# Two more places for the b gate's raw weights, and one cast tied behind another

## The chip, the cores and the metric

The kernel runs on one core of one Trainium2 chip. The metric is the device time of one execution in microseconds (us), input and output in the chip's memory; lower is better. The engines are named as in the profile: PE is TensorE (matrix products; PEld its weight loads), ACT is ScalarE, DVE is VectorE, POOL is GpSimd and SP is SyncE, whose queue issues most of the loads.

## The reference

Two layers work on 256 tokens of width 1024 in float32. In each, one normalised input h goes through a combined projection, whose parts feed two branches: a gated DeltaNet (branch a) and a differential softmax attention with eight heads (branch b). Each branch has a SiLU gate z, and a sigmoid gate of its own merges it. Cut to what matters here:

```
h = rmsnorm(x, norm_w[l]); proj = h @ w_in[l]
(q_a, k_a, v_a, ab_a, z_a, q_b, k_b, v_b, z_b, gate_a, gate_b) = split(proj)
y_a = gated_delta_branch(q_a, k_a, v_a, ab_a, z_a, ...)
y_b = diff_attention_branch(q_b, k_b, v_b, z_b, ...)   # softmax scores of heads 0 to 7
merged = sigmoid(gate_a) * (y_a @ w_pa[l]) + sigmoid(gate_b) * (y_b @ w_pb[l])
x = x + merged @ w_out[l]
```

## The kernel before

A projection is computed in pieces of 512 output columns. Its 1024 weight rows come in four pairs of 128 rows (`kp` = 0 to 3; the matmul steps are `kt` = 0 to 7, two for each pair). For one pair `weights` (L227) loads a raw tile of 128x1024 float32 (L247, on SP's queue), casts it on ACT to a rounded high part `hi` (L251), and subtracts that on DVE to get the low part `lo` (L253). `proj_tm` (L258) then makes, for each of two token tiles and two steps, three products: high activations by high weights (L267), by low weights (L268), and low activations by high weights (L269). That is twelve matmuls of 128x512 for a pair and 48 for a projection.

The raw tiles rotate through three places (`tag="raw", bufs=3`); a load can go when the subtraction of an earlier pair has read its place. High and low parts rotate through two buffers each ("the ring"): a cast can go when PE has finished the pair that lies there. A pair may be given a home of its own (`homes` in `weights`, `places` in `proj_tm`); its cast then waits only for its load and for that home. `first` names pairs with a home that are queued with high priority all the same. `later` ties the cast or the subtraction of a pair behind another instruction of the same engine. Nobody writes the order on an engine out in full: a scheduler simulates the instructions' times and puts each on its engine's queue when it is ready there, by priority. On the chip every queue then runs in that order, and an instruction that waits holds up those behind it.

The order of the work around the change is: zb, za, gb, ga (z gates and merging gates of the branches), each as two projections, so zb0, zb1, za0, za1, gb0, gb1, ga0, ga1. The attention of branch b is spread among them: for each head `scores` (L914 on PE; maxima on DVE, L922; exponentials on ACT, L924; combination on DVE, L930), `turn` (transposes, L941) and `attend` (weighted sum, L952, and its copy and squares on ACT, L956 and L958). Scores of heads 4 to 7 fall in za0, za1 and gb0. The rotated q and k lie in `qkT` (L463), one tile for heads 0 to 3 and one for heads 4 to 7, in two of the four places of the tag `p8`; the other two hold the activations `hT`. Each is 8 KB a partition. Once their scores are done, the two places of `qkT` come free. In gb1 and ga the kernel also weighs the DeltaNet's q-k products (L654, L686) and merges triangular blocks (`merges`: L776 needs the tile `T`, loaded on SP and POOL at L758, L790 the tile `U`), and the turned output of branch b then takes two places of `p8`.

Before the change the b gate has two homes in the room of `qkT`, `wgb[0]` for the high and low part of gb0's pair 2, and `wgb[1]` for those of gb1's pair 1 (L1062 to L1067). All its raw tiles go through the three ordinary places.

Of the kernel before, what the change touches and what calls it, by code (L numbers as in the profile page):

```python
# [8 lines left out]
F32 = mybir.dt.float32  # L9
F32R = mybir.dt.float32r  # L10
# [7 lines left out]
P = 128  # L18
# [31 lines left out]
def hybrid_encoder(  # L50
# [21 lines left out]
    def pool(name, bufs=1, space=None):  # L72
        kw = {} if space is None else {"space": space}
        return ctx.enter_context(tc.tile_pool(name=name, bufs=bufs, **kw))
# [3 lines left out]
    big = pool("big")  # L78
# [67 lines left out]
    def e4(name, tag):  # L146

        return [big.tile([P, NM, 512], F32, tag=tag, name=f"{name}_{i}", bufs=2) for i in range(2)]
# [72 lines left out]
    def pair(nm):  # L221
        return [big.tile([P, 2, 4, SEQ], F32R, tag="p8", name=f"{nm}_{i}", bufs=4) for i in range(2)]

    def behind(ins):
        return nullcontext() if ins is None else tc.issue_after(ins)

    def weights(w, c0, n, nm, homes=(None,) * 4, ahead=True, later=None, spare=(), held=None, turned=(), first=()):  # L227

        for kp in range(4):
            act, dve = (later or {}).get(kp, (None, None))
            act = mark[nm, act][0] if isinstance(act, int) else act
            with tc.high_priority(offset=HP) if ahead and (homes[kp] is None or kp in first) else nullcontext():
                if homes[kp] is not None:
                    hi, lo = homes[kp] if isinstance(homes[kp], list) else (homes[kp][:, 0], homes[kp][:, 1])
                else:
                    hi = wpool.tile([P, 2, 512], F32R, tag="hi", name=f"hi_{nm}{kp}", bufs=2)
                    lo = wpool.tile([P, 2, 512], F32R, tag="lo", name=f"lo_{nm}{kp}", bufs=2)  # L240
                if kp in spare:
                    raw = work.tile([P, 2, 512], F32, tag="w4a", name=f"raw_{nm}{kp}", bufs=2)
                else:
                    raw = wpool.tile([P, 2, 512], F32, tag="raw", name=f"raw_{nm}{kp}", bufs=3)
                load = (held or {}).get(kp)
                with behind(load):
                    mark["load", nm, kp] = (nc.scalar if load and load.engine != nc.sync.engine else nc.sync).dma_start(  # L247
                        out=raw[:, :, :n],
                        in_=w[kp * 256 : (kp + 1) * 256, c0 : c0 + n].rearrange("(k p) c -> p k c", p=P)).ins
                with behind(act):  # L250
                    high = (V.tensor_copy if kp in turned else S.copy)(hi[:, :, :n], raw[:, :, :n]).ins  # L251
                with behind(dve):
                    mark[nm, kp] = high, V.tensor_tensor(lo[:, :, :n], raw[:, :, :n],  # L253
                                                         hi[:, :, :n].bitcast(F32), ALU.subtract).ins
            for k in range(2):
                yield 2 * kp + k, hi[:, k, :n], lo[:, k, :n]

    def proj_tm(act, w, c0, n, evac, nm, places=(None,) * 4, spare=(), later=None, turned=(), between=None,  # L258
                banks=None, held=None, first=()):

        accs = (banks or banks2)(f"pp_{nm}")
        for kt, hi, lo in weights(w, c0, n, nm, places, later=later, spare=spare, turned=turned, held=held,
                                  first=first):
            for m in range(NM):
                ts_ = slice(m * P, (m + 1) * P)
                o = accs[m][:, :n]
                T.matmul(o, act[kt // 4][:, 0, kt % 4, ts_], hi, start=kt == 0, stop=False)  # L267
                T.matmul(o, act[kt // 4][:, 0, kt % 4, ts_], lo, start=False, stop=False)  # L268
                mark["proj"] = T.matmul(o, act[kt // 4][:, 1, kt % 4, ts_], hi, start=False,  # L269
                                        stop=kt == KT - 1).ins  # L270
                mark["done", nm, kt] = mark["proj"]
        if between:
            between()
        for m in range(NM):
            evac(m, accs[m][:, :n])

    def homes(tags, nm):

        for tag, n in tags:
            t_ = big.tile([P, n, 2, 2, 512], F32R, tag=tag, name=f"w{tag}_{nm}")  # L280
            for k in range(n):
                yield t_[:, k]
# [82 lines left out]
    for l in range(DEPTH):  # L365
# [12 lines left out]
        places = list(homes((("A", 1), ("ktm", 1), ("vtm", 1), ("B", 2)), f"vb{l}"))  # L378
# [4 lines left out]
        later, between, held = {}, None, {}  # L383
        if l == 0:
            later[0] = None, mark["norm", 0][1]

            def between(kt):
                if kt == 2:
                    held[1] = mark["square", 0, 0]
                    later[1] = mark["split", 0, 0]  # L390
                elif kt == 4:
                    tokens(1, mark["square", 0, 1])
                    held[2] = mark["vb00", 0][0]
                elif kt == 6:
                    prenorm(1, xt, wb, 0, (mark["split", 0, 1][0], mark["vb00", 2][1]))
                    later[3] = None, mark["norm", 1][1]
        else:
            later = {1: mark["norm", 0], 2: (mark["norm", 0][0], mark["split", 0, 0][1]), 3: mark["split", 0, 0]}
            mark["later"] = {0: mark["norm", 1], 1: mark["norm", 1]}
        for _ in proj_by_tile(hT, wl, C_VB, evac_v(0), f"vb{l}0", places, later=later,  # L400
                              spare=(1, 3) if l else (), held=held, between=between,
# [280 lines left out]
        def weigh_q(g, c, after):  # L682
            bv = B[:, c, 4 * g : 4 * g + 4]
            with tc.high_priority(offset=HP):
                gp = gram("kq", g, c, 1, after)
                mark["weighed"] = V.tensor_tensor(bv, gp.unsqueeze(2).to_broadcast([P, 4, 2, P]), bv, ALU.mult).ins  # L686
# [276 lines left out]
        def z_part(z, c_base, nm, i):  # L963
            def evac_z(m, ps):
                silu2(z[i][:, m, :], ps)
            proj_tm(hT, wl, c_base + 512 * i, 512, evac_z, f"{nm}{l}{i}",
                    banks=None if i or nm == "za" else banks2_c)
# [6 lines left out]
        for _ in proj_by_tile(hT, wl, C_VB + 512, evac_v(1), f"vb{l}1", places2, spare=range(4),  # L974
                              later={0: mark["split", 1, 1], 1: mark["split", 1, 1], 2: mark[f"k{l}0", 1],
                                     3: mark[f"k{l}0", 2]} if l else
                              {0: (mark["ab"], mark[f"k{l}0", 1][1]), 1: mark[f"k{l}0", 2],
                               2: mark[f"k{l}0", 3], 3: mark[f"k{l}1", 1]},
                              held={} if l else dict.fromkeys(range(2), mark[f"k{l}0", 1][0])):
# [61 lines left out]
                                                   zv[:, j, :], ALU.mult, ALU.mult)  # L1041
                    split_T(yT[i], ov, m, f"{nm}{i}", w=nw_)

        def gate(c_base, nm, tag, between=(None, None), places=((None,) * 4,) * 2, first=()):
            gt = []
            for i in range(2):
                def evac_g(m, ps, i=i):
                    if not gt:
                        gt.extend(e4(nm, tag))
                    S.activation(gt[i][:, m, :], ps, AF.Tanh, scale=0.5)  # L1050
                proj_tm(hT, wl, c_base + 512 * i, 512, evac_g, f"{nm}{i}", places[i], between=between[i],
                        first=first)
            return gt

        def branch(yT, w_, gt, nm, places=(None,) * 4):
            for i in range(2):
# [2 lines left out]
                    V.scalar_tensor_tensor(gs, gs, 1.0, ps, ALU.add, ALU.mult)  # L1059
                proj_tm(yT, w_, 512 * i, 512, evac_p, f"{nm}{i}", (None,) * 4 if i else places)  # L1060

        wgb = [t_.rearrange("p x b t -> p x (b t)").rearrange("p x (k c) -> p x k c", k=2)  # L1062
               for t_ in pair(f"wgb{l}")]
        gtb = gate(C_GB, f"gb{l}", "ev",
                   (lambda: attend(7, turn(7, es[7], place(34)), place(39)),
                    lambda: [weigh_q(n // 2, n % 2, place((39, 42, 44, 47)[n])) for n in range(4)]),
                   ((None, None, wgb[0], None), (None, wgb[1], None, None)), (1, 2))  # L1067
        r0 = small.tile([P, NM, NH], F32, tag="r0", name=f"r0{l}")
        V.reciprocal(r0, s_all[:, :, 0, :].rearrange("p h q -> p q h"))
        rb = small.tile([P, NM, NH], F32, tag="rb", name=f"rb{l}")  # L1070
# [10 lines left out]

        gate_yb(0)
        gta = gate(C_GA, f"ga{l}", "eo", (lambda: gate_yb(1), None))
        branch(ybT, w_pb[l], gtb, f"pb{l}")
        ch = [chunks(0), chunks(1)]
# [44 lines left out]
        def evac_o(i):  # L1130
            def evac(m, ps):
# [6 lines left out]
                later={2: mark[f"pa{l}0", 3], 3: mark[f"pa{l}1", 1]},  # L1138
                held={2: mark["load", f"pb{l}1", 1], 3: mark["load", f"pb{l}1", 3]})
# [4 lines left out]
                              later={0: mark[f"o{l}0", 1], 1: (mark[f"o{l}0", 1][0], mT_split[1]),  # L1144
                                     2: mT_split, 3: mT_split}, spare=(1, 3),
# [51 lines left out]
```

## Time and profile before

| | us |
|---|---|
| median of 3 runs | 769.4 |
| lowest, highest | 768.44, 772.19 |
| the profiled execution, its own time | 770.43 |
| its span in the profile | 768.7 |

| engine | busy us | share of the span |
|---|---|---|
| PE | 749.1 | 97% |
| DVE | 577.7 | 75% |
| ACT | 470.8 | 61% |
| POOL | 126.1 | 16% |

The profile records each instruction with its start and length, in us from the start of the span. A row of the timeline ends in brackets with how long the engine sat idle before it, and what ended that. Matmuls are pipelined: one of 128x512 is recorded as 0.39 us long, though they start 0.23 us apart. The mean clock granted to PE was 0.996 of full speed.

### The profile page before, as it was taken

How to read it: one execution, taken by the hardware profiler on the slowest of the kernel's cores; microseconds unless marked ns; L12 is line 12 of the kernel's file. 1: busy time of each engine (PE TensorE's matmuls, PEld its weight loads, DVE VectorE, ACT ScalarE, POOL GpSimd, SP SyncE). 2: the span in 40 equal slices, each digit the busy share in tenths (PEclk: the TensorE clock that was granted, in tenths of full speed). 3: DMA queues.
4: the chain of work that ended last, by engine and by line, in shares of the span. 5: the costliest groups of instructions: out<-in, count | busy, mean ns of one | idle time of the engine just before them, and what ended most of it. 6: DMA issues, size and time to landing. Idle time of an engine off the chain costs nothing.

```text
span 768.7 us, 13763 instructions
## 1 busy us (share of the span) xinstructions
PE 749.1 (97%) x5158; PEld 641.8 (83%) x5158; DVE 577.7 (75%) x1083; ACT 470.8 (61%) x1012; POOL 126.1 (16%) x187
## 2 busy tenths in 40 slices
PE   7999999999999999999999999999999889999996
PEld 4899889977877889988889889888787678998884
DVE  5696899999876763478577779999998458437782
ACT  5657675668766574645455668556776557565551
POOL 5100451112031111000010025202111310301000
PEclk9999999999999999999999999999999999999999
DMA  7762767775578242557674257768655934335641
GB/s 230 222 197 60 211 210 210 213 219 171 148 191 202 84 139 86 165 192 239 199 226 140 80 167 245 210 186 232 180 167 160 196 111 133 93 110 192 212 144 55
DMA packets 71795, 131.24 MB, mean 171 GB/s; under 512 B 12288, under 2 KB 12752, under 8 KB 71729
## 3 DMA queue, kind: packets, MB, share of 16 engines
q1 hardware_dynamic: 62718, 111.94, 48.7%
q0 software_dynamic: 6304, 15.15, 7.3%
q10 hardware_dynamic: 2706, 3.28, 1.3%
q8 instruction: 40, 0.66, 0.4%
q14 instruction: 27, 0.21, 0.1%
HBM read 123.44 MB, written 6.91 MB: 170 GB/s over the span
## 4 chain that ended last, share of the span: by engine, by line
PE 72%; DVE 13%; DMA 7%; ACT 4%; issue 3%; POOL 0%; SPq 0%; POOLq 0%; DVEq 0%
PE pp_vb L307 4%; DMA raw_gb<-in_w_in_dram 4%; PE pp_o L307 3%; PE pp_qk L268 2%; PE pp_qk L269 2%; PE pp_qk L267 2%; PE pf_v L323 2%; PE pf_k L327 2%; PE pf_v L327 2%; PE pf_k L325 2%; PE pf_v L325 2%; PE pf_k L323 2%; PE pp_ga L267 2%; PE pp_pb L269 2%; PE pp_ga L269 2%
## 5 line engine op out<-in xcount | busy, mean ns | idle before, releaser
L268 PE MATMUL pp_qk<-lo_qk,hT 128*128 128x512 f32 x128 | 50.9, 398 | 0.2
L269 PE MATMUL pp_qk<-hi_qk,hT 128*128 128x512 f32 x128 | 50.1, 391 | 0.0
L253 DVE TENSOR_TENSOR lo_qk<-raw_qk,hi_qk 128x1024 fp32r<-128x1024 f32 x32 | 40.2, 1257 | 9.7 <-ACT hi_qk L251 9.3
L267 PE MATMUL pp_qk<-hi_qk,hT 128*128 128x512 f32 x128 | 45.2, 393 | 0.0
L251 ACT CAST hi_qk<-raw_qk 128x1024 fp32r<-128x1024 f32 x28 | 29.4, 1050 | 23.5 <-PE pp_qk L269 11.1
L924 ACT ACTIVATE es<-sc,mx 128x256 f32<-128x256 f32 x64 | 29.6, 473 | 17.5 <-DVE mx L922 17.5
L253 DVE TENSOR_TENSOR lo_pb<-raw_pb,hi_pb 128x1024 fp32r<-128x1024 f32 x16 | 19.6, 1225 | 26.8 <-ACT hi_pb L251 26.8
L325 PE MATMUL pf_q<-hT,hi_q 128*128 128x256 f32 x128 | 36.2, 286 | 0.0
L323 PE MATMUL pf_q<-hT,hi_q 128*128 128x256 f32 x128 | 36.1, 287 | 0.0
L323 PE MATMUL pf_v<-hT,hi_v 128*128 128x256 f32 x128 | 35.9, 285 | 0.0
L325 PE MATMUL pf_v<-hT,hi_v 128*128 128x256 f32 x128 | 35.8, 284 | 0.0
L323 PE MATMUL pf_k<-hT,hi_k 128*128 128x256 f32 x128 | 35.7, 284 | 0.0
L325 PE MATMUL pf_k<-hT,hi_k 128*128 128x256 f32 x128 | 35.6, 283 | 0.0
L327 PE MATMUL pf_q<-hT,lo_q 128*128 128x256 f32 x128 | 34.9, 285 | 0.0
L327 PE MATMUL pf_v<-hT,lo_v 128*128 128x256 f32 x128 | 34.5, 288 | 0.0
L327 PE MATMUL pf_k<-hT,lo_k 128*128 128x256 f32 x128 | 34.4, 284 | 0.0
L552 DVE SCALAR_TENSOR_TENSOR cvq<-pf_q,cw,cvq 128x254 f32<-128x254 f32 (+1 forms) x64 | 29.9, 476 | 1.9 <-ACT cvq L548 1.4
L251 ACT CAST hi_pa<-raw_pa 128x1024 fp32r<-128x1024 f32 x16 | 16.9, 1055 | 22.2 <-PE pp_pa L269 16.0
L552 DVE SCALAR_TENSOR_TENSOR cvv<-pf_v,cw,cvv 128x254 f32<-128x254 f32 (+1 forms) x64 | 30.0, 477 | 0.1
L268 PEld LDWEIGHTS pp_qk<-lo_qk,hT 128*128 128x128 f32 x128 | 24.0, 188 | 7.2 <-DVE lo_qk L253 2.3
L552 DVE SCALAR_TENSOR_TENSOR cvk<-pf_k,cw,cvk 128x254 f32<-128x254 f32 (+1 forms) x64 | 28.5, 478 | 2.0 <-ACT cvk L548 1.3
L269 PEld LDWEIGHTS pp_qk<-hi_qk,hT 128*128 128x128 f32 x128 | 24.0, 188 | 4.9
(370 smaller groups left out, 2522.4 us busy)
## 6 DMA issues: line engine op xcount, KB each, us to landing
raw_qk<-in_w_in_dram SPq DMA_DIRECT2D x32, 512.0 KB, 3.8
raw_k<-in_w_in_dram SPq DMA_DIRECT2D x16, 512.0 KB, 4.9
raw_q<-in_w_in_dram SPq DMA_DIRECT2D x16, 512.0 KB, 3.7
raw_v<-in_w_in_dram SPq DMA_DIRECT2D x16, 512.0 KB, 3.8
raw_zb<-in_w_in_dram SPq DMA_DIRECT2D x16, 512.0 KB, 3.7
raw_za<-in_w_in_dram SPq DMA_DIRECT2D x16, 512.0 KB, 3.8
raw_gb<-in_w_in_dram SPq DMA_DIRECT2D x16, 512.0 KB, 5.6
raw_ga<-in_w_in_dram SPq DMA_DIRECT2D x16, 512.0 KB, 4.0
```

The lines of the kernel that those rows point to most:

```text
L251: high = (V.tensor_copy if kp in turned else S.copy)(hi[:, :, :n], raw[:, :, :n]).ins
L253: mark[nm, kp] = high, V.tensor_tensor(lo[:, :, :n], raw[:, :, :n], hi[:, :, :n].bitcast(F32), ALU.subtract).ins
L267: T.matmul(o, act[kt // 4][:, 0, kt % 4, ts_], hi, start=kt == 0, stop=False)
L268: T.matmul(o, act[kt // 4][:, 0, kt % 4, ts_], lo, start=False, stop=False)
L269: mark["proj"] = T.matmul(o, act[kt // 4][:, 1, kt % 4, ts_], hi, start=False, stop=kt == KT - 1).ins
L307: mark["proj"] = T.matmul(o, a_, w_, start=kt == 0 and a_ is ah and w_ is hi, stop=kt == KT - 1 and a_ is al).ins
L323: T.matmul(o, hi[:, cs], act[kt // 4][:, 0, kt % 4, :], start=first, stop=False, skip_group_check=True)
L325: T.matmul(o, hi[:, cs], act[kt // 4][:, 1, kt % 4, :], start=False, stop=False, skip_group_check=True)
L327: T.matmul(o, lo[:, cs], act[kt // 4][:, 0, kt % 4, :], start=False, stop=done, skip_group_check=True)
L552: V.scalar_tensor_tensor(ca[:, o0:o1], acc[:, b, o0 + sft : o1 + sft], cw[:, j, cb : cb + 1], ca[:, o0:o1], ALU.mult, ALU.add)
L924: S.activation(es[:, n, qt, :], spv[:, qt, :], AF.Exp, bias=mx[:, n, qt : qt + 1], accum_out=s_all[:, h, n, qt : qt + 1])
```

## The change

Of the two places of `qkT`, the first now takes `rgb`, the raw tiles of gb0's pairs 2 and 3 (through a new argument `raws`); they are no longer loaded into the three ordinary raw places. The high and low part of gb0's pair 2 go through the ring like those of the other pairs. The second place takes `wgb`, the high and low part of gb1's pair 1, as before. And in gb1 the cast of pair 1 on ACT is tied behind the cast of pair 0 (`later`), for the b gate only.

```
-    def weights(w, c0, n, nm, homes=(None,) * 4, ..., turned=(), first=()):
+    def weights(w, c0, n, nm, homes=(None,) * 4, ..., turned=(), first=(), raws={}):
...
-                if kp in spare:
+                if kp in raws:
+                    raw = raws[kp]
+                elif kp in spare:
...
-        def gate(c_base, nm, tag, between=(None, None), places=((None,) * 4,) * 2, first=()):
+        def gate(c_base, nm, tag, between=(None, None), places=((None,) * 4,) * 2, first=(),
+                 raws=({}, {})):
...
-                        first=first)
+                        later={1: (0, None)} if i and places[i][1] is not None else None,
+                        first=first, raws=raws[i])
...
-        wgb = [t_.rearrange("p x b t -> p x (b t)").rearrange("p x (k c) -> p x k c", k=2)
-               for t_ in pair(f"wgb{l}")]
+        rgb = big.tile([P, 2, 2, 512], F32, tag="p8", name=f"rgb{l}", bufs=4)
+        wgb = big.tile([P, 2, 2, 512], F32R, tag="p8", name=f"wgb{l}", bufs=4)
         gtb = gate(C_GB, f"gb{l}", "ev",
                    (lambda: attend(7, ...), lambda: [weigh_q(...) ...]),
-                   ((None, None, wgb[0], None), (None, wgb[1], None, None)), (1, 2))
+                   ((None,) * 4, (None, wgb, None, None)), (1,),
+                   ({2: rgb[:, 0], 3: rgb[:, 1]}, {}))
```

More of the change, by code (lines that the diff above doesn't have):

```diff
@@ L225, in behind, with weights @@
         return nullcontext() if ins is None else tc.issue_after(ins)
-    def weights(w, c0, n, nm, homes=(None,) * 4, ahead=True, later=None, spare=(), held=None, turned=(), first=()):
+    def weights(w, c0, n, nm, homes=(None,) * 4, ahead=True, later=None, spare=(), held=None, turned=(), first=(), raws={}):
         for kp in range(4):
@@ L258, in proj_tm @@
     def proj_tm(act, w, c0, n, evac, nm, places=(None,) * 4, spare=(), later=None, turned=(), between=None,
-                banks=None, held=None, first=()):
+                banks=None, held=None, first=(), raws={}):
         accs = (banks or banks2)(f"pp_{nm}")
         for kt, hi, lo in weights(w, c0, n, nm, places, later=later, spare=spare, turned=turned, held=held,
-                                  first=first):
+                                  first=first, raws=raws):
             for m in range(NM):
```

## The prediction

> **What bounds the kernel now.** I read the page first.
>
> ```profile
> PE 749.1 (97%) x5158; PEld 641.8 (83%) x5158; DVE 577.7 (75%) x1083; ACT 470.8 (61%) x1012; POOL 126.1 (16%) x187
> ...
> PE pp_vb L307 4%; DMA raw_gb<-in_w_in_dram 4%; PE pp_o L307 3%; PE pp_qk L268 2%; PE pp_qk L269 2%; PE pp_qk L267 2%; PE pf_v L323 2%; PE pf_k L327 2%; PE pf_v L327 2%; PE pf_k L325 2%; PE pf_v L325 2%; PE pf_k L323 2%; PE pp_ga L267 2%; PE pp_pb L269 2%; PE pp_ga L269 2%
> ```
>
> TensorE (PE) is busy for 749.1 of 768.7 us, so at most 20 us of waiting can be won anywhere. The second line is the chain that ended last: one group in it is a load, and it is the raw weights of the b gate. The chain in order of time says where (start, length, what):
>
> ```profile
> 220.28 5.94 DMA raw_gb<-in_w_in_dram
> ...
> 227.20 1.92 ACT es L924 x8
> ...
> 232.05 7.87 DMA raw_gb<-in_w_in_dram
> 239.94 1.06 ACT wgb L251
> ```
>
> Two loads in layer 0 lie on the chain, and ScalarE (ACT) is what waited for them. The windows view, cut at projections, says what that cost PE. Columns: stretch, length, busy time of PE, PEld, DVE, ACT, POOL, granted clock, DMA share, GB/s.
>
> ```profile
> 209.65:224.66 15.01, 15.01 (x82) 11.87 (x81) 12.75 (x25) 9.54 (x26) 2.37 (x4) 1.00 0.59 168
> 224.66:241.99 17.33, 15.35 (x81) 11.98 (x79) 9.43 (x17) 11.26 (x30) 6.90 (x12) 1.00 0.80 190
> 241.99:253.55 11.56, 10.84 (x180) 9.22 (x180) 6.61 (x9) 6.30 (x17) 3.15 (x2) 1.00 0.68 194
> 597.41:616.20 18.79, 15.36 (x82) 11.99 (x80) 9.43 (x17) 11.27 (x30) 6.90 (x12) 1.00 0.86 174
> 616.20:629.34 13.14, 12.42 (x180) 10.35 (x180) 6.60 (x9) 6.29 (x17) 3.14 (x2) 0.87 0.54 161
> 618.00:622.00 4.00, 4.00 (x12) 3.14 (x11) 1.23 (x1) 2.09 (x4) 0.00 (x0) 0.57 0.83 262
> ```
>
> The first row is za1 (the second za projection) of layer 0: 15.01 us, PE never idle. The second is gb0 (the first b-gate projection), with as many PE records: 17.33. The fourth is gb0 of layer 1: 18.79. Rows three and five are the same stretch of gb1 in the two layers, 11.56 and 13.14. The last row shows why they differ: between 618 and 622 the granted clock was 0.57. PE's timeline has these waits (in brackets, with what ended them):
>
> ```profile
> 230.04 0.74 PE L941 MATMUL at<-ident,es 128*128 128x128 f32 x4 [1.59 <-DVE es L930]
> ...
> 241.99 0.73 PE L267 MATMUL pp_gb<-hi_gb,hT 128*128 128x512 f32 x2 [0.40 <-ACT hi_gb L251]
> 243.44 0.50 PE L268 MATMUL pp_gb<-lo_gb,hT 128*128 128x512 f32 x1 [0.72 <-DVE lo_gb L253]
> ...
> 602.38 0.74 PE L941 MATMUL at<-ident,es 128*128 128x128 f32 x4 [1.17 <-DVE es L930]
> ...
> 616.20 0.73 PE L267 MATMUL pp_gb<-hi_gb,hT 128*128 128x512 f32 x2 [2.26 <-ACT hi_gb L251]
> ```
>
> So each layer loses time twice: before the turning of head 6's scores, and at the start of gb1. Both come from ACT's order, as two of its rows show:
>
> ```profile
> 226.24 1.05 ACT L251 CAST wgb<-raw_gb 128x1024 fp32r<-128x1024 f32 x1 [4.34 <-DMA raw_gb<-in_w_in_dram]
> ...
> 240.90 1.04 ACT L251 CAST hi_gb<-raw_gb 128x1024 fp32r<-128x1024 f32 x1
> ```
>
> ACT stood for 4.34 us at the cast of gb0's third pair, and head 6's exponentials (227.20 on the chain) queued behind it; VectorE then combined them late, and PE's transposes waited 1.59. At gb1 ACT cast the second pair first (239.94, right when its load landed: 232.05 + 7.87) and only then the first, at 240.90, which PE needed for 241.99.
>
> **The two early loads.** A raw load waits today for one of three places, freed by a VectorE subtraction:
>
> ```profile
> 214.59 0.37 SPq L247 DMA_DIRECT2D raw_gb<-in_w_in_dram  x1
> ...
> 220.28 0.37 SPq L247 DMA_DIRECT2D raw_gb<-in_w_in_dram  x1
> ```
> ```profile
> 219.03 1.22 DVE L253 TENSOR_TENSOR lo_za<-raw_za,hi_za 128x1024 fp32r<-128x1024 f32 x1
> ```
>
> The third pair's load left at 220.28 because the subtraction ended at 219.03 + 1.22 = 220.25. In the changed kernel pairs 2 and 3 of gb0 get a place of their own, the first room of the rotated q and k that comes free:
>
> ```profile
> 196.85 1.13 PE L914 MATMUL sc<-qkT 64*128 64x256 f32 x8
> ...
> 230.71 1.13 PE L914 MATMUL sc<-qkT 64*128 64x256 f32 x8
> ```
>
> Heads 0 to 3 use the first room; head 3's scores are the group at 196.85, so it is free near 198. (Head 7's, at 230.71, free the second, which the casts of gb1's second pair take as before.) On SyncE's queue the two loads come behind gb0's second pair, 214.59, so I put them near 215.0 and 215.4. They need no subtraction to have run, and nothing queued behind them on SyncE is due before 220.28. The place that comes free at 220.28, and the next one after gb0's first subtraction, go to gb1's first two pairs, of which one leaves at 232.05 today: some 9 us earlier. The 4.34 and the corresponding idle of ACT at gb1 go. The cost is DMA: 1 MB moves into za1, whose share is 0.59, out of gb0, whose share is 0.80 to 0.86. I cost it at nothing: what covers it is that nothing landing in za1 is needed within 5 us. If that cover is gone, the next victim is the T load that the triangular merge needs:
>
> ```profile
> 230.34 2.57 POOL L758 DMA_DIRECT2D T<-udr  x4
> ```
> ```profile
> T<-udr POOLq DMA_DIRECT2D x2, 64.0 KB, 6.7
> ```
> ```profile
> 248.40 1.47 PE L776 MATMUL y64p<-T,A 32*32 32x32 f32 x128
> ```
>
> The last of these four leaves near 232.3 and lands by 239.0; PE uses it at 248.40, or about 245 after the change. Six microseconds are spare, so this stays at zero.
>
> **Casts into the ring.** Pair 2 of gb0 loses its own home and goes, like its neighbours, through the two hi/lo buffers. So its cast must now wait until PE has finished pair 0, and pair 3's until pair 1 is done. The number of instructions doesn't change. The chain of such a handover is one cast and one subtraction, against PE's work on one pair (twelve matmuls):
>
> ```profile
> L251 ACT CAST hi_gb<-raw_gb x12: 1031/1046/1062, 220.4 to 621.6; 128x1024 fp32r<-128x1024 f32 x12
> L253 DVE TENSOR_TENSOR lo_gb<-raw_gb,hi_gb x12: 1218/1226/1226, 221.4 to 622.7; 128x1024 fp32r<-128x1024 f32 x12
> ```
> ```profile
> 226.47 0.39 PE L268 MATMUL pp_gb<-lo_gb,hT 128*128 128x512 f32 x1
> 226.70 0.39 PE L269 MATMUL pp_gb<-hi_gb,hT 128*128 128x512 f32 x1
> ```
>
> Chain: 1.05 + 1.23 = 2.28. Cover: 12 x 0.23 = 2.76, plus attention work of about 1 us (za1's 15.01 less 48 x 0.23, over four pairs). That is 0.5 to 1.5 us in hand, but head 7's four exponentials (1.92) and its maximum fall there too. The nearest row is za1's: all four pairs in the ring, the same attention work, VectorE busier (12.75 against 9.43), and PE idle 0.00. The other bound is a wait of 0.40, as at 241.99, in each of the four new handovers (pairs 2 and 3, two layers): 1.6. A gain from this edit alone is excluded, since a private home can only be ready sooner. I take 0.8, half of the bound, as za1 is the closer row.
>
> **The tied cast.** gb1's second pair is cast behind its first. Behind that cast on ACT queue only head 6's output copy and squares; VectorE's subtraction for that pair waits for it, and PE needs the pair a full 2.76 us after the first. Cost nothing. It makes the order that PE needs.
>
> **The sum.** Gain at gb0, against za1's 15.01: 17.33 - 15.01 = 2.32 and 18.79 - 15.01 = 3.78. (gb0 has one weighted sum more and one score group less than za1, a few tenths that I neglect.) Gain in gb1: 11.56 - 10.84 = 0.72 and 13.14 - 12.42 = 0.72 of idle time, and 13.14 - 11.56 = 1.58 of low clock. Together 9.12; less 0.8 gives 8.3. After gb1 the work follows PE, so the gain is kept. The profiled execution took 770.43 us (768.7 of span, 1.7 around it), 1.0 above the median 769.4; it would become 762.1, and the median 761.1.
>
> The clock term weighs on a rule. The trace has a full clock until 616.20, a PE wait of 2.26 and 0.72 more of idle time, and then 0.57; layer 0, with 0.40 and 0.72, has 1.00 in gb1. So I tie the 1.58 to the long wait. The Trainium skill ("TensorE: Matmul & The Clock Gate", section on what is actually happening in the clock gate) says that the clock halves after at least one idle window of about 3.4 us. By that rule no single wait here is long enough and the low clock need not go; the trace speaks for a lower limit. By the rule the gain would be estimated at 6.7.
>
> **Rivals.**
> - *The low clock stays* where it is, for reasons other than the wait: gain 8.3 - 1.6 = 6.7, 762.7. Against it: layer 0, same code, does without. This is what the rule above would make. Chance 0.08.
> - *A wait for PE takes the place of the wait for the load.* If ACT's order keeps pair 2's cast ahead of head 6's exponentials, as now, the cast waits until PE ends pair 0, near 228.3; the exponentials start at 229.4 instead of 227.20, and the transposes near 232.2 instead of 230.04. That loses 2.2 in each layer. What is won at gb1 stays: 0.40 + 0.72 + 2.26 + 0.72 + 1.58 = 5.7. Net 5.7 - 4.4 = 1.3, 768.1; with a low clock behind each longer wait (2 x 1.58), 771.3. For it: this is today's order. Against: with its room not free, that cast is no longer ready before the exponentials. Chance 0.17, no change.
> - *Slower: the ring is the new bound.* If a handover runs late behind the exponentials and the maximum, as long as layer 1's at 616.20 (2.26, the 0.72 of idle time in its gb1, and 1.58 of low clock: 4.56), in all four places, that is 18.2 against 9.1 gained: 778.5. It decides from 2.3 us per handover. Against: za1's idle 0.00. Chance 0.11.
> - *The change doesn't do what it says:* the new places come free only with head 7's scores, 230.71 + 1.13 = 231.84, instead of near 198. With the chain's 5.94 the load lands at 237.8, and cast and subtraction end at 240.1, where PE wants the pair near 233: 7.1 of wait and 1.58 of low clock, twice, 17.4 against 9.1: 777.7. Against: the room of heads 0 to 3 is free first. Chance 0.06.
>
> **How the numbers follow.** The forecast has 0.58. Its own range is 758.3 to 763: at the low end nothing is lost in the ring (9.1), each of the six waits hid another 0.16 (a matmul is recorded 0.39 long, at a pitch of 0.23), and the median falls as low as the fastest run shown, 768.44, or 1.0. Half a per cent, 3.85 us, is about what a measurement here can tell from no change: faster is below 765.6, slower above 773.2. Faster 0.58 + 0.08 = 0.66; same 0.17; slower 0.11 + 0.06 = 0.17. The range runs from 758.3 to 770.0, into the second rival, and leaves out the slower cases.
>
> **What would show it.** Right: loads into the new room issued between 209 and 224 in layer 0; no ACT wait for raw_gb over 1 us; the transposes of head 6 without a PE wait; gb1's first pair cast before its second; full clock in layer 1's gb1; gb0 near 15 us in both layers. Wrong: ACT waiting for PE at pair 2's cast with the exponentials behind it; PE waits on lo_gb inside gb0; or a merge waiting for T. A span won in gb but lost again before the output would mean that something behind gb does not follow PE.

## The result and the profile after

The changed kernel takes 761.3 us in the median (760.7 to 761.8, 4 runs) against 768.9 of the kernel before (766.0 to 772.2, 4 runs): ratio 0.9893, 95% interval 0.9864 to 0.9923. A second series of both gave 761.0 and 769.5. It is faster by 1%, as forecast (761.1). The profiled execution took 761.66 us. Its span is 759.9 against 768.7: 8.8 us less.

The page of the kernel after, its row for PE and the groups of the chain that ended last:

```profile
PE 745.7 (98%) x5158; PEld 640.3 (84%) x5158; DVE 575.6 (76%) x1083; ACT 471.0 (62%) x1012; POOL 124.2 (16%) x187
...
PE pp_o L309 1%; PE pp_gb L270 1%; PE pp_gb L269 1%; PE pp_ga L269 1%; PE pp_ga L271 1%; PE pp_gb L271 1%; PE pp_ga L270 1%; PE pp_pb L269 1%; PE pp_pb L270 1%; PE pp_pb L271 1%; PE po L880 1%; PE pp_pa L270 1%; PE pp_pa L271 1%; PE pp_pa L269 1%; PE pp_za L270 1%; PE pp_za L269 1%
```

The load of the b gate's raw weights is gone from the chain; the groups listed are PE's alone. This profile follows the chain back only to 561.77, so it says this of layer 1; for layer 0 the rows below must say it. PE's instructions are the same in number (5158), and its idle time fell from 19.6 to 14.2 us. The windows view of the kernel after, cut as before: za1 of layer 0, gb0 of both layers, and the stretch from the start of gb1 to the first `zt` matmul (L792) of both layers (columns as in the prediction):

```profile
209.73:224.71 14.98, 14.98 (x82) 11.84 (x81) 13.24 (x27) 11.50 (x34) 2.40 (x4) 1.00 0.59 172
224.71:239.66 14.95, 14.95 (x81) 12.25 (x80) 10.21 (x17) 12.11 (x32) 6.92 (x12) 1.00 0.90 180
594.44:609.35 14.91, 14.91 (x81) 12.26 (x80) 10.23 (x17) 12.15 (x32) 6.92 (x12) 1.00 0.82 170
239.66:250.21 10.55, 10.55 (x181) 8.99 (x179) 5.67 (x8) 4.55 (x11) 3.15 (x2) 1.00 0.67 200
609.35:619.96 10.61, 10.61 (x186) 9.06 (x188) 5.64 (x8) 4.53 (x11) 3.15 (x2) 1.00 0.68 201
```

PE is busy for the whole of every stretch, at full clock. gb0 went from 17.33 and 18.79 to 14.95 and 14.91. For the last two rows the same cut of the kernel before reads

```profile
241.99:253.86 11.87, 11.15 (x180) 9.22 (x180) 6.88 (x10) 6.30 (x17) 3.15 (x2) 1.00 0.66 189
616.20:629.66 13.46, 12.74 (x181) 10.36 (x181) 6.89 (x10) 6.29 (x17) 3.14 (x2) 0.87 0.53 157
```

so 1.32 was won there in layer 0. In layer 1 the cut after lies 0.07 behind the first `zt` matmul, which starts at 619.89; the stretch up to it is 10.54 long, and 2.92 was won. ACT's timeline of the kernel after in layer 0:

```profile
223.36 0.47 ACT L926 ACTIVATE es<-sc,mx 128x256 f32<-128x256 f32 x1 [1.41 <-DVE mx L924]
...
228.54 1.05 ACT L253 CAST hi_gb<-rgb 128x1024 fp32r<-128x1024 f32 x1 [0.20 <-PE pp_gb L271]
...
231.48 0.48 ACT L926 ACTIVATE es<-sc,mx 128x256 f32<-128x256 f32 x1 [1.41 <-DVE mx L924]
...
236.66 1.05 ACT L253 CAST hi_gb<-raw_gb 128x1024 fp32r<-128x1024 f32 x1 [1.04 <-PE pp_gb L271]
237.62 1.05 ACT L253 CAST wgb<-raw_gb 128x1024 fp32r<-128x1024 f32 x1
...
242.84 1.05 ACT L253 CAST hi_gb<-raw_gb 128x1024 fp32r<-128x1024 f32 x1 [1.43 <-DMA raw_gb<-in_w_in_dram]
```

Head 6's exponentials start at 223.36 instead of 227.20. gb0's pair 2 is cast after them, and gb1's pair 0 ahead of pair 1. Before these two casts ACT now stands for PE (1.04), which costs nothing. It still stands once for a load, 1.43 us before the cast of gb1's last pair (1.53 in layer 1), but PE does not wait for that pair. On SP's queue the first load into the new places, with the second right behind it:

```profile
200.07 0.37 SPq L249 DMA_DIRECT2D raw_za<-in_w_in_dram  x1
200.49 0.46 SPq L249 DMA_DIRECT2D rgb<-in_w_in_dram  x1
```

They leave in za0, right behind a load of za1's weights, and the first 28 us before its cast.

### The profile page after: what moved, and what is told of

It reads as the page before. It is cut to its first block, busy times and chain, and to the rows that moved or that the text cites. A ratio compares the mean times of both kernels' runs of the same rounds, so it can differ in the third digit from the quotient of the medians.

```text
span 759.9 us, 13759 instructions
## 1 busy us (share of the span) xinstructions
PE 745.7 (98%) x5158; PEld 640.3 (84%) x5158; DVE 575.6 (76%) x1083; ACT 471.0 (62%) x1012; POOL 124.2 (16%) x187
## 5 line engine op out<-in xcount | busy, mean ns | idle before, releaser
L255 DVE TENSOR_TENSOR lo_pb<-raw_pb,hi_pb 128x1024 fp32r<-128x1024 f32 x16 | 19.6, 1227 | 23.0 <-ACT hi_pb L253 22.9
L255 DVE TENSOR_TENSOR lo_ga<-raw_ga,hi_ga 128x1024 fp32r<-128x1024 f32 x16 | 19.5, 1219 | 20.9 <-ACT hi_ga L253 20.9
```

## The experiments

Theory A: the change helps because of the order of ACT's queue. A cast stood there whose load was late, and work with its data ready stood behind. Theory B: the weights themselves came too late for PE, and the two early places cure that. Each kernel was timed against the kernel before on the same chip.

**Without the tie.** The changed kernel without the line `later={1: (0, None)} ...` in `gate`.

> The change without the tied cast: the two early places stay. Theory A (it is ACT's in-order queue: what counts is which work stands behind a cast whose data are late): the wait before head 6's transposes goes (2.3 us of gb0 in layer 0, about 1.5 in layer 1). In the new order gb1's second pair is cast ahead of head 7's exponentials, with its load long landed, so it costs them one cast, 1.05 us, and no wait for a load; gb1's first pair is cast in time. So nearly all of the gain: ratio to before 0.989 to 0.992, 761 to 763 us, and the tie is worth 0 to 2 us once the loads are early. Rival (the tie is what mends gb1, whatever the loads do): the waits of 0.40 and 2.26 at the start of gb1 and layer 1's low clock stay; ratio 0.994 to 0.996, about 765.5.

Measured: 760.6 us against 769.5, ratio 0.9883 (0.9853 to 0.9912), the same as with the tie. ACT's timeline:

```profile
229.97 1.05 ACT L253 CAST wgb<-raw_gb 128x1024 fp32r<-128x1024 f32 x1
...
231.37 0.47 ACT L926 ACTIVATE es<-sc,mx 128x256 f32<-128x256 f32 x1 [0.35 <-DVE mx L924]
```

gb1's pair 1 is cast ahead of head 7's exponentials, in a gap where ACT waits for VectorE anyway (0.35 of idle is left where the changed kernel has 1.41, at 231.48). Its load had left at 222.64, and ACT does not wait for it. So with early loads the tie is worth nothing that can be measured; the rival falls. This is not a test of the early loads alone, since gb0's pair 2 has no home here either. Early loads with both homes kept were not run.

**The tie alone.**

```
 # kernel before, in gate
...
+    later={1: (0, None)} if i and places[i][1] is not None else None,
...
```

> The kernel before with the tied cast alone; the only difference in ACT's order is that gb1's pair 0 is cast before pair 1. Theory A: gb1's first load landed well before ACT stood waiting for the second one (it left at 228.58, the other at 232.05), so the cast moves from 240.90 to about 237 and PE waits neither 0.40 nor 2.26 for it, and layer 1 keeps its full clock (1.58). Head 6's transposes still wait 1.59 and 1.17. Gain 0.40 + 0.72 + 2.26 + 0.72 + 1.58 = 5.7 at most; ratio 0.992 to 0.995, 763 to 765 us. Rival (the loads are late, so the order does not matter): PE then waits for the second pair instead, and the time stays within 0.3% of before.

Measured: 766.2 against 769.5, ratio 0.9955 (0.9932 to 0.9977). PE's timeline has one wait left in each layer's b gate:

```profile
230.38 0.74 PE L941 MATMUL at<-ident,es 128*128 128x128 f32 x4 [1.52 <-DVE es L930]
...
602.59 0.74 PE L941 MATMUL at<-ident,es 128*128 128x128 f32 x4 [1.46 <-DVE es L930]
```

The waits at gb1 and the low clock are gone, and those before head 6's transposes stayed, as A has it. The median gained 3.3 us, somewhat less than was expected (766.2 where 763 to 765 had been put); the profiled span gained 4.9.

**The order alone.** Both ties on the kernel before, no new place.

```
+    mark["es", h, n] = S.activation(es[:, n, qt, :], ...).ins
...
+    later=({1: (0, None)} if i else {2: (mark["es", 6, 0], None)}) if ... else None,
```

> The kernel before with two ties and no new place: gb0's pair 2 is cast behind head 6's exponentials, and gb1's pair 1 behind pair 0. The loads stay where they were, one later than the other. Theory A (order of ACT's queue): pair 2's load lands near 226.2, after the exponentials end near 225.2, and PE needs the pair only near 232.9, so the waits go without any early load: all of the change's gain, ratio 0.988 to 0.991, 760.5 to 762.5 us, gb0 near 15 us in both layers. Theory B (the data come too late, and the two places cure that): PE now waits in gb for hi_gb or wgb, at pair 2 of gb0 or at pair 1 of gb1 whose load landed at 239.9; gain below 6 us, ratio 0.993 or more.

Measured: 762.0 against 769.5, ratio 0.9910 (0.9877 to 0.9943). ACT and PE:

```profile
226.25 1.06 ACT L251 CAST wgb<-raw_gb 128x1024 fp32r<-128x1024 f32 x1 [0.93 <-DMA raw_gb<-in_w_in_dram]
...
240.77 1.05 ACT L251 CAST wgb<-raw_gb 128x1024 fp32r<-128x1024 f32 x1 [4.41 <-DMA raw_gb<-in_w_in_dram]
```
```profile
243.13 0.50 PE L268 MATMUL pp_gb<-wgb,hT 128*128 128x512 f32 x1 [0.35 <-DVE wgb L253]
...
610.72 0.50 PE L268 MATMUL pp_gb<-lo_gb,hT 128*128 128x512 f32 x1 [0.76 <-DVE lo_gb L253]
```

The first cast starts at 226.25, as in the kernel before (226.24): the load is as late as ever, and nobody minds, since the exponentials now go first. ACT still stands 4.41 us for the second load, and PE loses 0.35 in layer 0 and 0.76 in layer 1. Nearly the whole gain is had without any early load, so B falls as an account of the gain. The early places are worth what lies between this kernel and the changed one, about 1 us by the medians of different series; the intervals overlap.

**No homes.** The kernel before, with its two private homes taken away and nothing in their place.

```
-    wgb = [...]
...
-    ((None, None, wgb[0], None), (None, wgb[1], None, None)), (1, 2))
+    ((None,) * 4, (None,) * 4))
```

> The kernel before with its two private homes in the room of q and k taken away and nothing put in their place: every pair of the b gate goes through the three raw places and the ring. Theory A (order of ACT's queue): a pair without a home cannot be cast before PE has let go of the ring, so no cast stands ahead of head 6's exponentials any more, and gb1's pairs are cast in turn. The gain then comes from taking the homes away, not from the new places: within about 2 us of the changed kernel, ratio 0.988 to 0.992, 760.5 to 763.5 us, with waits under 1 us where a raw load lands late (the order-only kernel had 0.35 and 0.76). Theory B (early places are needed): PE waits for pairs whose loads leave only after 228, 2 us or more in each layer; ratio 0.993 or more.

Measured: 762.0 against 769.5, ratio 0.9906 (0.9882 to 0.9931). ACT, and 15 us of gb0 in each layer:

```profile
228.97 1.04 ACT L251 CAST hi_gb<-raw_gb 128x1024 fp32r<-128x1024 f32 x1 [0.15 <-PE pp_gb L269]
```
```profile
225.00:240.00 15.00, 15.00 (x82) 12.34 (x81) 9.57 (x17) 11.28 (x31) 6.91 (x12) 1.00 1.00 224
595.00:610.00 15.00, 15.00 (x82) 12.29 (x81) 9.52 (x16) 11.22 (x31) 6.90 (x12) 1.00 1.00 219
```

Less code does what the change does, within 1 us. Pair 2 cannot be cast before PE lets go of the ring (228.97), and so it never stands in front of the exponentials. Its load is no earlier than in the kernel before: it leaves at 221.54 instead of 220.28. The home was the harm: it let the cast into the queue early, where it waited for its load.

**All in the ring, and one place.** The changed kernel without the home of gb1's pair 1 (`(None,) * 4` for both projections), and the changed kernel with `{2: rgb[:, 0]}` only.

> The changed kernel with the early raw places, but without the home of gb1's pair 1 and so without the tied cast: all eight pairs of the b gate go through the ring. Theory A, with za1 as the model (four pairs in the ring, PE never idle): no new wait, ratio 0.987 to 0.991, 760 to 762 us, as with the home. Rival (the home in the second room carries part of the gain, since gb1 also holds the q-k products and the first merge): a wait of 0.4 to 1 us at pair 1 or 2 of gb1 in each layer, 762 to 763.5 us.

> The changed kernel with one new place instead of two: only gb0's pair 2 is loaded early, pair 3 goes through the three ordinary places. Theory A: pair 2 was the cast on which ACT stood, so one place gives the whole gain, 760 to 762.5 us, ratio 0.987 to 0.991; pair 3's load then takes the place freed at 220.3 and lands well before 233. Theory B (the number of places counts): the loads of gb1 slide back by one place, to near 228 and 232, and half of the gain is lost, 764 to 766 us.

> The changed kernel itself, as the measure for the three others on the same chip: 760.5 to 762 us, ratio 0.987 to 0.992.

Measured on one chip: 761.1 (ratio 0.9897, 0.9875 to 0.9920) without the home, 760.8 (0.9905, 0.9872 to 0.9938) with one place, 761.0 (0.9893, 0.9871 to 0.9915) for the changed kernel itself. PE has no wait in gb in any of the three. With early loads, neither the home in the second room nor the second early place carries anything measurable.

**The other tie alone.** Only gb0's pair 2 behind head 6's exponentials.

> The kernel before with the other of the two ties alone: gb0's pair 2 is cast behind head 6's exponentials, while gb1's pair 1 is still cast ahead of pair 0. If the two waits add up (order-only 7.5 us, tie-only 3.3 us by the medians), this is worth 3.5 to 4.5 us: 765 to 766.5 us, with no wait before head 6's transposes and with the waits at the start of gb1. Against adding up: with the first wait gone PE reaches gb1 some 2 us earlier while its loads are tied to VectorE's subtractions, so the wait at gb1 may grow by as much, lower the clock in both layers, and take the gain back: then 768 to 771 us.

Measured: 773.1 against 768.9, ratio 1.0044 (1.0016 to 1.0073): slower, and by more than expected. ACT, PE, and two windows:

```profile
240.01 1.04 ACT L251 CAST wgb<-raw_gb 128x1024 fp32r<-128x1024 f32 x1 [6.05 <-DMA raw_gb<-in_w_in_dram]
```
```profile
242.05 0.73 PE L267 MATMUL pp_gb<-hi_gb,hT 128*128 128x512 f32 x2 [3.05 <-ACT hi_gb L251]
243.50 0.80 PE L268 MATMUL pp_gb<-lo_gb,hT 128*128 128x512 f32 x1 [0.72 <-DVE lo_gb L253]
...
617.04 0.73 PE L267 MATMUL pp_gb<-hi_gb,hT 128*128 128x512 f32 x2 [1.62 <-ACT hi_gb L251]
618.49 0.80 PE L268 MATMUL pp_gb<-lo_gb,hT 128*128 128x512 f32 x1 [0.72 <-DVE lo_gb L253]
```
```profile
242.00:250.00 8.00, 7.23 (x21) 5.54 (x22) 3.42 (x4) 4.52 (x10) 0.00 (x0) 0.57 0.74 211
616.00:624.00 8.00, 6.24 (x24) 4.90 (x25) 3.97 (x4) 5.52 (x12) 0.00 (x0) 0.79 0.61 184
```

The first wait is gone, but gb1's pair 1 is still cast first, and its load still lands near 240. PE only comes to that point sooner: its wait grew from 0.40 to 3.05 in layer 0, and the clock fell in both layers, where it had fallen in layer 1 alone. In layer 1 the wait went from 2.26 to 1.62. The two ties do not add up; without the second, the first moves the wait in layer 0 and adds a low clock there. The profiled execution, 771.12, is one of the quicker of this kernel (769.35 to 775.49), and its span is only 0.7 above that of the kernel before. Why the slower ones take up to 4 us more was not traced.

**Late loads.** The changed kernel with the loads into the new places held on SP behind the T loads (`load = mark["T"]` for pairs in `raws`).

> The changed kernel with the two loads into the new places held on SP's queue behind the T loads of the triangular merge, so that they leave near 228.5 instead of 200.5. It prices the fourth rival of the prediction (places that come free late). Both theories: they land near 233 to 234, cast and subtraction follow by 2.3, and PE wants pair 2 near 232.7, so PE waits 2.5 to 4 us in each layer, and head 7's exponentials stand behind that cast on ACT. If a wait of that length lowers the clock, as 2.26 + 0.72 seemed to do in layer 1 of before, 1.6 us more in a layer. Ratio to before 0.994 to 1.003, 764 to 771 us. If the loads were early by much more than needed and the queue on ACT does not matter, the time stays at 761 to 762.

Measured: 773.5 against 769.5, ratio 1.0060 (1.0038 to 1.0083). ACT, PE and PE's clock:

```profile
235.35 1.04 ACT L255 CAST hi_gb<-rgb 128x1024 fp32r<-128x1024 f32 x1 [5.52 <-DMA rgb<-in_w_in_dram]
```
```profile
236.45 0.73 PE L271 MATMUL pp_gb<-hi_gb,hT 128*128 128x512 f32 x2 [2.30 <-ACT hi_gb L255]
237.71 0.50 PE L272 MATMUL pp_gb<-lo_gb,hT 128*128 128x512 f32 x1 [0.53 <-DVE lo_gb L257]
```
```profile
238.00:242.00 4.00, 4.00 (x14) 3.06 (x13) 1.14 (x4) 0.42 (x3) 0.00 (x0) 0.60 0.86 182
614.00:618.00 4.00, 4.00 (x12) 3.12 (x13) 1.95 (x5) 2.24 (x7) 0.00 (x0) 0.57 0.64 146
```

The loads left at 228.41, into a stretch where the DMA engines are full (a share of 1.07 from 228 to 236), and the first landed near 235.3. Here the data are late for PE itself, in both layers: 2.37 and 0.53 of waits in layer 1, and in layer 0 another 0.59 and 0.53 for pair 3. The sign turns: 12 us lie between this kernel and the changed one. So B is a real mechanism; it only was not what ailed the kernel before.

**Loads at 215**, one run: held behind the load of gb0's pair 1.

> The changed kernel with the two early loads held on SP's queue behind the load of gb0's pair 1, so that they leave near 215, where the prediction had put them, instead of 200.5. They are needed by 228.5. All theories: no wait in gb that the changed kernel has not, span 759 to 761. It would show a wait only if the loads slowed the T loads or gb1's first loads behind them.

They left at 217.68, later than meant. The run took 762.83 us, with a span of 761.1, no PE wait in gb, and 20.0 us from the start of gb0 to the first merge (226.6 to 246.6), as in the changed kernel (224.7 to 244.7). This execution was behind by 1.9 us before gb0 began. So loads at 200 and at 218 were both early enough for PE in gb.

## Why the prediction was right, point by point

*The bound and the sum.* The two waits and the low clock were the terms, and all went. gb0 gave 2.38 and 3.88 (forecast 2.32 and 3.78). The gb1 stretch gave 1.32 and 2.92 (forecast 0.72 and 0.72 + 1.58). That is 10.5 instead of 9.12 in the b gate, a little more than the low end of the forecast's range took in (9.12 and six hidden tails of 0.16, 10.1). The span gained only 8.8. The first `zt` matmul comes 3.65 us earlier in layer 0, but layer 1's gb0 starts only 2.97 earlier; the `zt` of layer 1 comes 9.77 earlier and the end 8.8. Of that last 1.0, one wait is seen, which the kernel before does not have:

```profile
712.68 0.50 PE L270 MATMUL pp_pa<-lo_pa,yaT 128*128 128x512 f32 x1 [0.52 <-DVE lo_pa L255]
```

Of the 0.7 lost before layer 1's gb0, two other such waits of PE make 0.45: 0.21 at 400.83 (L509) and 0.24 at 573.77 (L943). They vary: a second profile of the changed kernel has 0.77 at the first and none at the second. Where the rest went was not traced. So misses cancelled: the b gate gave 1.4 more, the 0.8 for the ring was not needed, and some 1.7 was given back where the prediction let everything follow PE. The mechanism held; that the median came within 0.2 us of the forecast is in part luck.

*The ring.* I took 0.8 off for new waits between 0 and 1.6. It was 0: PE does not wait in the b gate, and not even with all eight pairs in the ring. za1 was the right row to go by.

*The early loads.* The place was right (the room of heads 0 to 3), the time was not: 200.49 instead of 215. I had the loads queue on SP in the order of the code; the scheduler put them where head 3's scores free the room. It made no difference. The load of gb1's pair 1 leaves at 222.75 instead of 232.05, the 9 us earlier that I had put. Of the signs named, two did not come: the loads did not leave between 209 and 224, and ACT still waits over 1 us for a raw tile, for gb1's last pair.

*Cause and cure.* The prediction saw ACT's order as the cause, and that was shown. But it counted on the early loads to end ACT's standing, and on the tie for the order at gb1. The runs say otherwise: the order alone cures both waits but for 0.35 and 0.76, taking away the homes alone cures both with the loads as late as before, and with early loads the tie does nothing. The prediction also ruled out a gain from pair 2's way through the ring alone, "since a private home can only be ready sooner". The reason fails: being ready sooner is what put the cast in front of the exponentials, and with both homes taken away the kernel gained 7.5 us (762.0 against 769.5). The ring stood in the sum as a cost, and with both homes gone it is enough for nearly the whole gain. Taking away pair 2's home alone was not run. The early loads are worth about 1 us by the medians.

*The rivals.* The low clock went with the waits, as the trace had suggested. No cast kept its place ahead of head 6's exponentials. The ring did not bind. The fourth, loads too late, was priced at 777.7; the late-loads kernel took 773.5, with waits of 2.30, 0.53, 0.59 and 0.53 in layer 0 where 7.1 had been put, in part because the loads left at 228.4 and not at 231.8.

## What to carry to other kernels

On an engine whose queue runs in order, look behind a waiting instruction and not only at it: the cost was not the late load but the ready exponentials behind it, and reordering two casts won nearly all of what the whole change won. A private buffer is not free of harm: here it took away the wait that kept an instruction behind more urgent work. Mend all the waits of one chain or check that the last one is mended: curing the first alone made this kernel 0.4% slower than leaving both.

## What the runs showed of the hardware

PE's granted clock fell to about half after waits of PE that were close together. With 2.26 and 0.72 (before, layer 1), 2.30 and 0.53 or 2.37 and 0.53 (late loads), and 3.05 and 0.72 (other tie, layer 0) it read 0.57 to 0.60 over windows of 4 or 8 us. With 1.62 and 0.72 (other tie, layer 1) it read 0.79 over 8 us, but 0.53 from 618 to 621.4 and 1.00 after 622: the fall was as deep and shorter than the window. After 0.40 and 0.72, after 0.76 alone, or after 1.59, 1.52 or 1.46 alone, it stayed at full speed. The Trainium skill ("TensorE: Matmul & The Clock Gate", section on what is actually happening) asks for an idle window of about 3.4 us; here some 2.3 us of idle time, split by two matmuls, was enough.
